# Computing the second row tile's queries, compressed branch and half of its window units beside the last projection chunk

## The chip, the cores and the metric

The kernel runs on one core of a Trainium2 chip. The metric is the device time of one launch in microseconds. Before the change three runs took 1413.13, 1410.7 and 1417.88 us; their median is 1413.13 us. A separate, profiled execution took 1414.72 us.

## What is computed

One transformer block over 1024 positions and 1024 channels, in float32. The normalised input is multiplied with one wide matrix `w_in`; its columns give the parts of two attentions. Attention A has eight heads with dilated windows. Attention B has eight query heads in two groups and three branches per query: a compressed branch (63 pooled keys), a selected branch (the eight best blocks of 64 keys, chosen from the compressed branch's scores) and a local window branch (512 keys back). Cut to what matters here:

```
qa, ka, va, qb, kc, vc, ksl, vsl, kwn, vwn, gl = split_columns(h @ w_in)
p_cmp = masked_softmax(qb @ k_cmp);  o_cmp = p_cmp @ v_cmp
score = overlap(p_cmp) + forced;     idx = top_k(score, 8)
o_sel = softmax over the selected blocks of qb @ ksl, times vsl
o_win = softmax over the last 512 keys of qb @ kwn, times vwn
ob    = gate0 * o_cmp + gate1 * o_sel + gate2 * o_win
h     = x + concat(rms_norm(oa), rms_norm(ob)) @ w_out
out   = rms_norm(h + relu(rms_norm(h) @ w_up)**2 @ w_down)
```

The selected branch needs the compressed branch of the same rows (for the top eight) and the keys and values `ksl`, `vsl`. The window branch needs neither.

## The kernel before

**Stages.** Phase one projects `w_in` in eleven chunks of 256 columns (one has 280) and runs attention A between them. Its order is a list, the string `P1` (line 28): `a0` to `a3` are attention A's head pairs, `kv0`, `qk1`, `v1`, `kw0`, `qb0` and so on are projection chunks, `X` opens attention B's buffers, `kb1` builds the window keys. Near its end stand `Q7` (load and stack the queries of the first row tile), `W7` (its window branch), `C7` (its compressed branch) and, last, `ks0`, the chunk with the selected branch's keys and values. Phase two is the rest of attention B with the output projection, phase three the feed-forward part.

**Order of the work.** The positions are eight row tiles of 128, taken in the order of `ORD` (line 31): tile 5 first, tile 7 second, tile 6 third. The program is written in one order, and a scheduler that runs a model of the engines puts each engine's instructions in an order of its own by priority: a smaller number goes first when it is ready. Chunks are written under `later(LATE)` (line 935), which adds 1000, so what is written after a chunk goes ahead of it where it can, and the chunk's matmuls fill up. Each engine, and the DMA queue of SP with it, then runs its list in order.

**A unit** is one head of one row tile in one branch (`attend`, line 504). It has score matmuls (lines 418, 420), a masked minimum on VectorE (429), an exponential on ScalarE (434), a split into two fp16 halves (448, and 450 on POOL or 452 on VectorE), a DMA that transposes both halves (453) and the matmuls with the values (468 to 470, "PV" below). Up to `DEPB` = 4 units wait for their PV (`retire`, line 485). Row buffers `ns`, halves `hl` and transposed halves `pt` have three slots each; phase two adds a few from the pool `bpp`.

**Around the change.** `q_load` (744) fetches a tile's queries, `q_build` (748) stacks them, `cmp_stages` (755) gives the compressed branch as c1 (matmuls 763 to 766, maximum 775, shift 777, exponential 778), c3 (four transposes, copy 784) and c4 twice (matmuls 795, copy 796, then some thirteen short VectorE steps, 804 to 819). For tile 5 these take slots of `ns` (`big`, line 147). After `ks0`, `wp` and `ht` close, the PSUM pool `ps1` is replaced by `ps3`, `bpp` opens, `build_kb(0)` (949) makes the selected keys, and the loop of line 968 goes over the tiles: first `load_wo` for four rows of `w_out`, then, beside tile n's units, tile n+1's queries and compressed branch at fixed unit counts (`STG`, line 32), then tile n's window and selected branches. Tile 5 has no window branch left there.

**Fillers.** The output projection is cut into pieces. Every unit of attention B adds a rate to a credit (`RATE`, line 39: 0.2 for tile 5, 0.5 for tile 7), and each full credit lets one piece in (`pump`, 876). The credit is set to zero in line 956, just ahead of the loop.

**Large buffers.** The pool `stp` has four slots. At the end of phase one they hold projected columns, afterwards the four pairs of residual rows (`hres`, line 943).

Of the kernel before, what the change touches and what calls it, by code (L numbers as in the profile page):

```python
# [9 lines left out]
F32 = mybir.dt.float32  # L10
# [8 lines left out]
T = 1024  # L19
D = 1024  # L20
NT = 8
# [3 lines left out]
NEG = -1e30  # L25
EPS = 1e-6
PSCALE = 4096.0
P1 = "a0 kv0 qk1 c0 a1 c1 qk2 v1 a2 qk3 kw0 qb0 qb1 a3 X G kb1 Q7 W7 C7 ks0"
CUT = 0
ISS = 0  # L30
ORD = [5, 7, 6, 4, 3, 2, 1, 0]
# [25 lines left out]
def build(tc, A, out):  # L57
# [89 lines left out]
    def big(name="ns", hl=False):  # L147
        if hl:
            return atp[0].tile([128, T], F32, name=name, tag="hl", bufs=3)
        return wk.tile([128, T], F32, name=name, tag="ns", bufs=3)  # L150
# [588 lines left out]
        return bpp.tile(shape, dt, name=name, bufs=bufs)  # L739

    fbn = {}
    Q2 = []

    def q_load(i):
        QR[i] = big("qr0")[:, :512] if i == ORD[0] and "qr" in FB else bpp.tile([128, 512], F32, name="qr", bufs=1)
        sp.dma_start(QR[i], qbd[i])

    def q_build(i):
        q = fb(i, [128, 2, 4, 128], F32R, "qb", 2)
        q2 = Q2[ORD.index(i) % 2]  # L750
        r = QR[i]
        q_stacks(q[:, 0], q[:, 1], q2, [r[:, j * 128:(j + 1) * 128] for j in range(4)])
        QB[i] = (q, q2)

    def cmp_stages(i):
        st = {}

        def c1():
            q, q2 = QB[i]
            ps = bank("S", [128, 512], 3).rearrange("p (h c) -> p h c", c=64)  # L760
            ps = ps.rearrange("p (g j) c -> p j g c", g=2)
            for j in range(4):
                pe.matmul(ps[:, j], identb, cmask[:, i, None, :].to_broadcast([128, 2, 64]), start=True, stop=False)
                for g in range(2):
                    pe.matmul(ps[:, j, g], q2[:, g, j], kcs[:, g], start=False, stop=False)
                    pe.matmul(ps[:, j, g], q[:, g, j], kcs[:, g], start=False, stop=g == 1)
            ps = ps.rearrange("p j g c -> p g j c")
            s = big("cs0")[:, :512].rearrange("p (h c) -> p h c", h=8) if i == ORD[0] and "cs" in FB else bpp.tile([128, 8, 64], F32, name="cs", tag="cs", bufs=1)
            st["s"] = s
            if not CM:  # L770
                dve.tensor_add(s.rearrange("p (g j) c -> p g j c", g=2), ps, cmask[:, i, None, None, :].to_broadcast([128, 2, 4, 64]))
            m = fb(i, [128, 1, 8], F32, "cm", 2)
            st["m"] = m
            x = ps if CM else s.rearrange("p (g j) c -> p g j c", g=2)
            dve.tensor_reduce(m[:, 0].rearrange("p (g j) -> p g j", g=2), x, axis=AX.X, op=OP.max)
            dve.tensor_scalar(m[:, 0], m[:, 0], -1e29, None, op0=OP.max)
            dve.tensor_sub(s.rearrange("p (g j) c -> p g j c", g=2), x, m[:, 0].rearrange("p (g j) -> p g j", g=2)[:, :, :, None].to_broadcast([128, 2, 4, 64]))
            act.activation(s, s, AF.Exp)

        def c3():  # L780
            s = st["s"].rearrange("p h c -> p (h c)")
            ps = transposes([s[:, j * 128:(j + 1) * 128] for j in range(4)])
            pt = big("cpt0")[:, :512].rearrange("p (h c) -> p h c", h=4) if i == ORD[0] and "cs" in FB else bpp.tile([128, 4, 128], F32, name="cpt", bufs=1)
            act.activation(pt, ps, AF.Copy)
            st["pt"] = pt

        def c4(g):
            if g == 0:
                if i == ORD[0] and "cs" in FB:
                    st["e"] = big("ce0")[:, :648].rearrange("p (g a b) -> p g a b", g=2, a=2)  # L790
                else:
                    st["e"] = bpp.tile([128, 2, 2, 162], F32, name="ce", tag="cs", bufs=1)
            ps = bank("O", [128, 512], 1)[:, :324].rearrange("p (a b) -> p a b", a=2)
            for j in range(2):
                pe.matmul(ps[:, j], st["pt"][:, 2 * g + j], vc[:, g], start=True, stop=True)
            act.activation(st["e"][:, g], ps, AF.Copy)
            if g == 0:
                return
            e = st["e"].rearrange("p g a b -> p (g a) b")
            sc = cs2.tile([128, 2, 2, 16], F32, name="csc", bufs=2)  # L800
            mx = cs2.tile([128, 8], F32, name="cmx", bufs=2)
            im = cs2.tile([128, 8, 16], F32, name="cim", bufs=1)
            rd = cs2.tile([128, 2, 4, 2], F32, name="crd", bufs=2)
            dve.tensor_scalar(rd[:, 0], e[:, :, 128:130], 1e-30, None, op0=OP.max)
            dve.reciprocal(rd[:, 0], rd[:, 0])
            dve.tensor_mul(im.rearrange("p (a b) s -> p a b s", a=4),
                           e[:, :, 130:162].rearrange("p a (b s) -> p a b s", b=2),
                           rd[:, 0, :, :, None].to_broadcast([128, 4, 2, 16]))
            dve.tensor_reduce(sc[:, 0], im.rearrange("p (g h) s -> p g s h", g=2), axis=AX.X, op=OP.add)
            OC[i] = fb(i, [128, 8, 64], F32, "oc", 3)  # L810
            dve.tensor_mul(rd[:, 1], rd[:, 0], gate[:, i, 0:24:3].rearrange("p (a b) -> p a b", a=4))
            pool.tensor_mul(OC[i].rearrange("p (a b) d -> p a b d", a=4),
                            e[:, :, 0:128].rearrange("p a (b d) -> p a b d", b=2),
                            rd[:, 1, :, :, None].to_broadcast([128, 4, 2, 64]))
            dve.tensor_add(sc[:, 0], sc[:, 0], addt[:, i, None, :].to_broadcast([128, 2, 16]))
            for g in range(2):
                dve.max(mx, sc[:, 0, g])
                dve.match_replace(sc[:, 1, g], mx, sc[:, 0, g], NEG)
            dve.tensor_scalar(sc[:, 1], sc[:, 1], -1.0, NEG, op0=OP.mult, op1=OP.add)
            for g in range(2):  # L820
                SB[i, g] = sc[:, 1, g]

        return c1, c3, lambda: c4(0), lambda: c4(1)

    def b_attend(i, br):
        n0 = max(0, i - 4)
        if br == 0:
            OB[i] = wop.tile([128, 8, 64], F32, name="ob", bufs=3)

        def f(br, h):  # L830
            g, j = divmod(h, 4)
            q, q2 = QB[i]
            if h == 0:
                OT[i, br] = fb(i, [128, 8, 65], F32, "ot", 2)
            k = kb[br][:, g].rearrange("p a b -> p (a b)")
            a, n = (0, i + 1) if br == 0 else (n0, i + 1 - n0)
            u = dict(i=i, h=h, q=q[:, g, j], q2=q2[:, g, j], k=k[:, a * 128:], n=n,
                     v=lambda t: V["kw" if br else "ks"][:, a + t, g], ev=OT[i, br][:, h - 1:h + 1], e=h % 2)
            if br:
                u["tab"] = wint[:, (5 - n) * 128:]  # L840
            else:
                u["sc"] = SB[i, g]
            return u

        for h in range(8):
            u = f(br, h)
            if h == 7:
                u["done"] = lambda: b_done(i, br)
            attend(u)
# [40 lines left out]
    for step in P0:  # L890
        if step == "X":
# [13 lines left out]
            ctmp = big()  # L905
            addt = bqp.tile([128, NT, 16], F32, name="addt")
            Q2.append(q2_tile(bqp, "qb20"))
            sp.dma_start(ctmp[:, :512], A["cmask"].rearrange("p a b -> p (a b)"))
            dve.tensor_copy(cmask.rearrange("p a b -> p (a b)"), ctmp[:, :512])
            sp.dma_start(addt, A["addt"])  # L910
# [12 lines left out]
        if step == "C7":  # L923
            for f in cmp_stages(ORD[0]):
                f()
            continue
        k, j = step[:-1], int(step[-1])
        if k == "a":
            a_pair(j)
# [10 lines left out]
    ps1_close()  # L940
    pst["pool"], ps3_close = mkpool("ps3", space=PSUM)
    pst["second"] = 1
    hres += [stp.tile([128, 2, T], F32, name="st") for j in range(4)]
    bpp, bpp_close = mkpool("bpp", side="right")
    Q2.append(q2_tile(bpp, "qb21"))
    for tag in ("ns", "hl", "pt"):
        xtra[tag] = (bpp, 0)
    kb[0] = bpp.tile([128, 2, NT, 128], F32R, name="kb0")
    build_kb(0)
    if "Q7" not in P0:  # L950
        q_load(ORD[0])
        q_build(ORD[0])
    if "C7" not in P0:
        for f in cmp_stages(ORD[0]):
            f()
    credit[0] = 0.0

    eng = dict(P=mybir.EngineType.PE, A=mybir.EngineType.Activation, D=mybir.EngineType.DVE, G=mybir.EngineType.Pool, S=mybir.EngineType.SP)
# [9 lines left out]
    for n, i in enumerate(ORD):  # L968
        if n == 0:
            load_wo(range(4))  # L970
        if n + 1 < NT:
            q_load(ORD[n + 1])
            jobs = (lambda i=ORD[n + 1]: q_build(i),) + cmp_stages(ORD[n + 1])
            for k, f in zip(STG, jobs):
                waiting.append([k, f])
        if n or "W7" not in P0:
            b_attend(i, 1)
        b_attend(i, 0)
    retire(0)
# [339 lines left out]
```

## Time and profile before

| | |
|---|---|
| median of three runs | 1413.13 us |
| the profiled execution's own time | 1414.72 us |
| its span, first to last instruction | 1412.9 us |
| matmuls on TensorE (PE) | busy 1313.4 us, 93% |
| weight loads on TensorE (PEld) | busy 1110.6 us, 79% |
| VectorE (DVE) | busy 970.4 us, 69% |
| ScalarE (ACT) | busy 650.3 us, 46% |
| GpSimd (POOL) | busy 512.0 us, 36% |

Busy shares are means over stages with different limits, and a matmul's record covers its whole way through the array, so that records of successive matmuls overlap. What a stage allows is read from the stretch itself: the idle time of each engine there, the granted clock of TensorE (1.00 is 2.4 GHz, and a mean below it means that part of the stretch ran at 1.2 GHz), and the chain of waits.

### The profile page before, as it was taken

To read this page: it belongs to the slowest core of one execution; us is meant where nothing else is said; L and a number is where in the kernel's file an instruction comes from. 1 tells how busy PE (TensorE), PEld (TensorE's weight loads), DVE (VectorE), ACT (ScalarE), POOL (GpSimd) and SP (SyncE) were. 2 spreads that over 40 slices of the span, in tenths; PEclk is the share of its full clock that TensorE was granted. 3 is DMA by queue.
4 is the path that set the end of the run, shared out by engine and by line. 5 is a ranking of instruction groups with operands and counts; after the bars stand their busy time and mean duration, and the time that the engine had idled before them with its cause. 6 is when DMAs were issued, how large, how long until landed. Compare 5 with 4: busy or idle time off the path is not lost.

```text
span 1412.9 us, 23742 instructions
## 1 busy us (share of the span) xinstructions
PE 1313.4 (93%) x8891; PEld 1110.6 (79%) x8891; DVE 970.4 (69%) x1953; ACT 650.3 (46%) x1212; POOL 512.0 (36%) x724
## 2 busy tenths in 40 slices
PE   7999999998987999899778999999999999999996
PEld 6788989888976777677656888888888888788885
DVE  6664565773458876878587667677767667776767
ACT  7462755872557866898553222222222212222216
POOL 3445473664445665577542110011111001111115
PEclk9999999999898999999999999999999999999998
DMA  6265382985538986686311121112111111111113
GB/s 189 68 113 120 87 185 51 206 184 145 93 107 180 172 152 129 143 157 96 82 30 34 56 59 46 45 46 60 45 60 46 59 41 50 55 50 61 45 46 134
DMA packets 265747, 131.68 MB, mean 93 GB/s; under 512 B 220064, under 2 KB 240544, under 8 KB 265632
## 3 DMA queue, kind: packets, MB, share of 16 engines
q1 hardware_dynamic: 265488, 129.90, 40.0%
q8 instruction: 70, 1.15, 0.3%
q14 instruction: 45, 0.37, 0.1%
q10 hardware_dynamic: 144, 0.26, 0.0%
HBM read 68.26 MB, written 8.39 MB: 54 GB/s over the span
## 4 chain that ended last, share of the span: by engine, by line
PE 57%; DVE 16%; DMA 8%; issue 7%; POOL 6%; ACT 5%; SPq 1%; DVEq 0%; POOLq 0%; ACTq 0%
PE S L1124 8%; PE S L1125 7%; PE S L1126 7%; PE F L335 3%; PE F L336 3%; PE F L337 3%; DMA u<-in_w_down_dram 3%; PE O L1064 2%; PE O L1063 2%; PE T L1065 2%; PE T L1063 2%; PE T L1064 2%; PE O L1065 2%; PE S L418 2%; DVE c L1071 1%
## 5 line engine op out<-in xcount | busy, mean ns | idle before, releaser
L1073 POOL TENSOR_TENSOR ul<-c,uh 128x512 fp32r<-128x512 f32 x64 | 92.5, 1454 | 557.8 <-ACT uh L1072 555.9
L1127 DVE SCALAR_TENSOR_TENSOR st<-S,r,st 128x512 f32<-128x512 f32 (+1 forms) x257 | 185.8, 742 | 70.3 <-PE S L1126 69.7
L1124 PE MATMUL S<-dn,uh 128*128 128x512 f32 (+1 forms) x514 | 203.2, 396 | 9.6 <-DVE c L1110 5.9
L1126 PE MATMUL S<-dn,ul 128*128 128x512 f32 (+1 forms) x514 | 200.6, 391 | 0.8 <-POOL ul L1073 0.8
L1125 PE MATMUL S<-dn,uh 128*128 128x512 f32 (+1 forms) x514 | 200.8, 391 | 0.0
L335 PE MATMUL F<-wh,hh 128*128 128x256 f32 (+1 forms) x576 | 167.2, 292 | 6.1 <-DVE st L214 3.2
L336 PE MATMUL F<-wl,hh 128*128 128x256 f32 (+1 forms) x576 | 166.5, 289 | 2.3 <-DVE wl L95 2.3
L337 PE MATMUL F<-wh,hl 128*128 128x256 f32 (+1 forms) x576 | 165.4, 288 | 0.0
L1124 PEld LDWEIGHTS S<-dn,uh 128*128 128x128 f32 x514 | 97.2, 189 | 37.8 <-DVE c L1110 12.2
L434 ACT ACTIVATE ns<-ns,mn 128x640 f32<-128x640 f32 (+7 forms) x152 | 110.7, 747 | 35.1 <-POOL mn L433 21.7
L335 PEld LDWEIGHTS F<-wh,hh 128*128 128x128 f32 x576 | 110.7, 193 | 8.2 <-DVE st L214 3.6
L450 POOL TENSOR_TENSOR hl<-ns,hl 128x640 f16<-128x640 f32 (+5 forms) x67 | 105.5, 1575 | 30.9 <-ACT hl L448 24.9
L1126 PEld LDWEIGHTS S<-dn,ul 128*128 128x128 f32 x514 | 97.0, 189 | 22.0 <-POOL ul L1073 1.5
L336 PEld LDWEIGHTS F<-wl,hh 128*128 128x128 f32 x576 | 111.3, 193 | 3.7 <-DVE wl L95 3.1
L1125 PEld LDWEIGHTS S<-dn,uh 128*128 128x128 f32 x514 | 97.4, 190 | 19.2
L337 PEld LDWEIGHTS F<-wh,hl 128*128 128x128 f32 x576 | 111.0, 193 | 0.5
L448 ACT ACTIVATE hl<-ns 128x640 f16<-128x640 f32 (+5 forms) x115 | 91.2, 802 | 5.8 <-DMA pt<-hl 5.0
L468 PE MATMUL O<-v,pt 128*128 128x65 f16 x694 | 77.3, 195 | 15.9 <-DMA pt<-hl 13.4
L1081 ACT ACTIVATE c<-T 128x512 f32<-128x512 f32 x15 | 9.0, 599 | 172.2 <-PE S L1125 172.2
L468 PEld LDWEIGHTS <-pt 128*128 128x128 f16 x694 | 63.9, 99 | 27.6 <-DMA pt<-hl 17.4
L418 PE MATMUL S<-kb,qb 128*128 128x384 f32 (+3 forms) x192 | 72.9, 385 | 12.6 <-DVE mn L429 8.9
L433 POOL TENSOR_SCALAR mn<-mn 128x1 f32<-128x1 f32 x130 | 43.7, 336 | 96.4 <-DVE mn L429 81.2
(372 smaller groups left out, 3625.1 us busy)
## 6 DMA issues: line engine op xcount, KB each, us to landing
u<-in_w_down_dram SPq DMA_DIRECT2D x64, 256.0 KB, 2.8
wr<-in_w_in_dram SPq DMA_DIRECT2D x44, 256.0 KB, 2.9
r<-in_w_up_dram SPq DMA_DIRECT2D x32, 256.0 KB, 2.7
st<-in_x_dram SPq DMA_DIRECT2D x8, 512.0 KB, 5.9
wor<-in_w_out_dram SPq DMA_DIRECT2D x16, 256.0 KB, 3.5
cA<-in_w_up_dram SPq DMA_DIRECT2D x16, 256.0 KB, 2.8
cB<-in_w_up_dram SPq DMA_DIRECT2D x16, 256.0 KB, 2.6
ns<-in_xT_dram SPq DMA_DIRECT2D x7, 512.0 KB, 5.1
```

The costliest lines, as they stand in the source:

```text
L335: pe.matmul(ps, hh[:, k, ts], hi, start=k == 0, stop=False)
L336: pe.matmul(ps, hh[:, k, ts], lo, start=False, stop=False)
L337: pe.matmul(ps, hl[:, k, ts], hi, start=False, stop=k == KD - 1)
L418: pe.matmul(ps[:, :w], u["q"], u["k"][:, cs], start=True, stop=False)
L434: u["exp"] = act.activation(ns[:, :n * 128], ns[:, :n * 128], AF.Exp, scale=-1.0, bias=mn[:, j:j + 1])
L450: pool.tensor_sub(lo, p, hi)
L468: pe.matmul(ps, ph, v[:, 64:129], start=t == 0, stop=False)
L1073: pool.tensor_sub(lo, a, f32(hi))
L1124: pe.matmul(ps, uh[:, ts], wd[:, 0, cs], start=j == 0, stop=False)
L1125: pe.matmul(ps, uh[:, ts], wd[:, 1, cs], start=False, stop=False)
L1126: pe.matmul(ps, ul[:, ts], wd[:, 0, cs], start=False, stop=j == 1)
L1127: dve.scalar_tensor_tensor(o[:, cs], ps, r2[:, t:t + 1], o[:, cs], op0=OP.mult, op1=OP.add)
```

## The change

`P1` gets three steps ahead of `ks0`. `QN` loads and stacks the queries of tile 7, `CN` computes its compressed branch, `WN` its window branch for heads 0 to 3. Heads 4 to 7 are written after `build_kb(0)` and before the credit is set to zero. The loop then prepares tile n+1 only from n = 1 on and leaves out tile 7's window branch. For this, tile 7's stacked queries and its outputs (`EX`) lie in two slots of `stp`; the residual rows are allotted in the order 2, 3, 1, 0; the second `q2` tile moves from `bpp` to `bqp`, a pool of phase one; the compressed branch of both tiles takes `ns` slots; `cm` moves to `cs2`, and `crd` has one buffer instead of two. Cut to its core:

```diff
-P1 = "a0 kv0 qk1 c0 a1 c1 qk2 v1 a2 qk3 kw0 qb0 qb1 a3 X G kb1 Q7 W7 C7 ks0"
+P1 = "a0 kv0 qk1 c0 a1 c1 qk2 v1 a2 qk3 kw0 qb0 qb1 a3 X G kb1 Q7 W7 C7 QN CN WN ks0"
...
     def q_load(i):
-        QR[i] = big("qr0")[:, :512] if i == ORD[0] and "qr" in FB else bpp.tile([128, 512], F32, name="qr", bufs=1)
+        QR[i] = big("qr0")[:, :512] if i in ORD[:2] else bpp.tile([128, 512], F32, name="qr", bufs=1)
...
     def q_build(i):
-        q = fb(i, [128, 2, 4, 128], F32R, "qb", 2)
+        if i == ORD[1]:
+            q = stp.tile([128, 2, 4, 128], F32R, name="st")
+        else:
+            q = fb(i, [128, 2, 4, 128], F32R, "qb", 2)
...
-            rd = cs2.tile([128, 2, 4, 2], F32, name="crd", bufs=2)
+            rd = cs2.tile([128, 2, 4, 2], F32, name="crd", bufs=1)
...
-    def b_attend(i, br):
+    def b_attend(i, br, heads=range(8)):
...
             Q2.append(q2_tile(bqp, "qb20"))
+            Q2.append(q2_tile(bqp, "qb21"))
...
+        if step == "QN":
+            q_load(ORD[1])
+            ex = stp.tile([128, 1032], F32, name="st")
+            EX.append(ex[:, 0:520].rearrange("p (h d) -> p h d", d=65))
+            EX.append(ex[:, 520:1032].rearrange("p (h d) -> p h d", d=64))
+            q_build(ORD[1])
+            continue
+        if step == "CN":
+            for f in cmp_stages(ORD[1]):
+                f()
+            continue
+        if step == "WN":
+            b_attend(ORD[1], 1, range(4))
+            continue
...
-    hres += [stp.tile([128, 2, T], F32, name="st") for j in range(4)]
+    rows = {j: stp.tile([128, 2, T], F32, name="st") for j in (2, 3, 1, 0)}
+    hres += [rows[j] for j in range(4)]
     bpp, bpp_close = mkpool("bpp", side="right")
-    Q2.append(q2_tile(bpp, "qb21"))
...
     build_kb(0)
...
+    b_attend(ORD[1], 1, range(4, 8))
     credit[0] = 0.0
...
-        if n + 1 < NT:
+        if 0 < n < NT - 1:
             q_load(ORD[n + 1])
...
-        if n or "W7" not in P0:
+        if n > 1:
             b_attend(i, 1)
         b_attend(i, 0)
```

## Rows read from the trace of the kernel before

**Rows 1.** The page: busy time of each engine over the span.

```profile
PE 1313.4 (93%) x8891; PEld 1110.6 (79%) x8891; DVE 970.4 (69%) x1953; ACT 650.3 (46%) x1212; POOL 512.0 (36%) x724
```

**Rows 2.** By stretch: length, busy PE, PEld, DVE, ACT, POOL (instructions), PE clock, DMA.

```profile
...
366.00:382.00 16.00, 13.80 (x127) 13.14 (x127) 8.83 (x30) 11.62 (x28) 9.24 (x17) 0.76 0.70 129
382.00:405.50 23.50, 23.50 (x195) 23.49 (x193) 6.67 (x24) 8.06 (x21) 10.19 (x33) 0.94 0.22 29
405.50:420.50 15.00, 9.31 (x99) 6.55 (x97) 12.27 (x33) 10.78 (x21) 6.17 (x13) 1.00 0.80 251
420.50:440.50 20.00, 16.34 (x135) 13.92 (x135) 14.79 (x31) 15.11 (x23) 8.04 (x8) 0.74 0.75 141
440.50:460.00 19.50, 15.47 (x187) 13.14 (x188) 18.48 (x56) 15.78 (x29) 12.54 (x15) 1.00 0.86 181
540.00:600.00 60.00, 50.72 (x497) 39.60 (x495) 45.47 (x123) 43.85 (x77) 31.47 (x38) 1.00 0.69 135
...
```

**Rows 3.** Chain that ended last, 405 to 427 us: start, duration, what.

```profile
...
409.65 5.20 DMA qr<-qbd
...
```

**Rows 4.** The same chain, 440 to 460 us: first and last of 63 pieces.

```profile
...
440.31 0.92 ACT ns L434
...
458.57 0.39 PE S L418
...
```

**Rows 5.** PE, timeline: start, duration, what; counts are each instruction's.

```profile
...
353.96 0.60 PE L360 MATMUL T<-c_ident,qr 128*128 128x128 f32 x4
354.32 0.36 PE L336 MATMUL F<-wl,hh 128*128 128x256 f32 x1
...
374.33 0.34 PE L337 MATMUL F<-wh,hl 128*128 128x256 f32 x1
...
376.62 0.33 PE L763 MATMUL S<-cmask,identb 128*128 128x128 bf16 x1
...
380.15 0.26 PE L468 MATMUL O<-v,pt 128*128 128x65 f16 x1
...
382.05 0.56 PE L335 MATMUL F<-wh,hh 128*128 128x256 f32 x1
...
391.98 0.71 PE L795 MATMUL O<-vc,cpt 128*128 128x162 f32 x4
392.42 0.39 PE L337 MATMUL F<-wh,hl 128*128 128x256 f32 x1
...
456.75 0.20 PE L468 MATMUL O<-v,pt 128*128 128x65 f16 x1 [1.05 <-DMA pt<-hl]
...
457.21 0.42 PE L418 MATMUL S<-kb,qb 128*128 128x384 f32 x1
...
457.88 0.34 PE L418 MATMUL S<-kb,qb 128*128 128x384 f32 x1
...
```

**Rows 6.** VectorE, timeline: one window unit, and ends of c4's steps for tile 5.

```profile
...
396.57 0.17 DVE L804 TENSOR_SCALAR crd<-ce 128x8 f32<-128x8 f32 x1 [2.76 <-ACT ce L796]
...
399.84 0.18 DVE L819 TENSOR_SCALAR csc<-csc 128x32 f32<-128x32 f32 x1
...
438.06 0.55 DVE L429 CUSTOM_DVE_ANT_0 nsx<-S,wint 128x384 f32<-128x384 f32 x1
...
438.77 0.48 DVE L429 CUSTOM_DVE_ANT_0 nsx<-S,wint,mn 128x256 f32<-128x256 f32 x1 [0.15 <-PE O L795]
...
451.77 0.81 DVE L452 SCALAR_TENSOR_TENSOR hl<-ns,hl 128x640 f16<-128x640 f32 x1
...
```

**Rows 7.** The tile qb: the second query split on VectorE (min/median/max ns).

```profile
...
L383 DVE SCALAR_TENSOR_TENSOR qb<-T,qb x8: 694/695/695, 357.8 to 648.3; 64x512 fp32r<-64x512 f32 x8
...
```

**Rows 8.** SP's queue, waits 366 to 410 us: total, times, longest.

```profile
...
SPq L453 <- PE O L470: 24.3, 2, 21.6
...
```

**Rows 9.** SP's queue, timeline of the same stretch.

```profile
...
407.49 1.17 SPq L681 DMA_DIRECT2D oat<-oad  x2
...
```

**Rows 10.** Line 709 of the output projection: durations ns min/median/max, first and last start.

```profile
...
L709 PE MATMUL F<-woh,mh x128: 387/395/796, 420.5 to 707.5; 128*128 128x512 f32 x128
...
```

More of the change, by code (lines that the diff above doesn't have):

```diff
@@ L741, in build @@
     fbn = {}
-    Q2 = []
+    Q2, EX = [], []
     def q_load(i):
-        QR[i] = big("qr0")[:, :512] if i == ORD[0] and "qr" in FB else bpp.tile([128, 512], F32, name="qr", bufs=1)
+        QR[i] = big("qr0")[:, :512] if i in ORD[:2] else bpp.tile([128, 512], F32, name="qr", bufs=1)
         sp.dma_start(QR[i], qbd[i])
     def q_build(i):
-        q = fb(i, [128, 2, 4, 128], F32R, "qb", 2)
+        if i == ORD[1]:
+            q = stp.tile([128, 2, 4, 128], F32R, name="st")
+        else:
+            q = fb(i, [128, 2, 4, 128], F32R, "qb", 2)
         q2 = Q2[ORD.index(i) % 2]
@@ L767, in c1 @@
             ps = ps.rearrange("p j g c -> p g j c")
-            s = big("cs0")[:, :512].rearrange("p (h c) -> p h c", h=8) if i == ORD[0] and "cs" in FB else bpp.tile([128, 8, 64], F32, name="cs", tag="cs", bufs=1)
+            s = big("cs0")[:, :512].rearrange("p (h c) -> p h c", h=8) if i in ORD[:2] else bpp.tile([128, 8, 64], F32, name="cs", tag="cs", bufs=1)
             st["s"] = s
@@ L771, in c1 @@
                 dve.tensor_add(s.rearrange("p (g j) c -> p g j c", g=2), ps, cmask[:, i, None, None, :].to_broadcast([128, 2, 4, 64]))
-            m = fb(i, [128, 1, 8], F32, "cm", 2)
+            m = cs2.tile([128, 1, 8], F32, name="cm", bufs=2)
             st["m"] = m
@@ L782, in c3 @@
             ps = transposes([s[:, j * 128:(j + 1) * 128] for j in range(4)])
-            pt = big("cpt0")[:, :512].rearrange("p (h c) -> p h c", h=4) if i == ORD[0] and "cs" in FB else bpp.tile([128, 4, 128], F32, name="cpt", bufs=1)
+            pt = big("cpt0")[:, :512].rearrange("p (h c) -> p h c", h=4) if i in ORD[:2] else bpp.tile([128, 4, 128], F32, name="cpt", bufs=1)
             act.activation(pt, ps, AF.Copy)
@@ L788, in c4 @@
             if g == 0:
-                if i == ORD[0] and "cs" in FB:
+                if i in ORD[:2]:
                     st["e"] = big("ce0")[:, :648].rearrange("p (g a b) -> p g a b", g=2, a=2)
@@ L809, in c4 @@
             dve.tensor_reduce(sc[:, 0], im.rearrange("p (g h) s -> p g s h", g=2), axis=AX.X, op=OP.add)
-            OC[i] = fb(i, [128, 8, 64], F32, "oc", 3)
+            OC[i] = EX[1] if i == ORD[1] else fb(i, [128, 8, 64], F32, "oc", 3)
             dve.tensor_mul(rd[:, 1], rd[:, 0], gate[:, i, 0:24:3].rearrange("p (a b) -> p a b", a=4))
@@ L823, in cmp_stages @@
         return c1, c3, lambda: c4(0), lambda: c4(1)
-    def b_attend(i, br):
+    def b_attend(i, br, heads=range(8)):
         n0 = max(0, i - 4)
-        if br == 0:
+        if br == 0 and 0 in heads:
             OB[i] = wop.tile([128, 8, 64], F32, name="ob", bufs=3)
@@ L833, in f @@
             if h == 0:
-                OT[i, br] = fb(i, [128, 8, 65], F32, "ot", 2)
+                OT[i, br] = EX[0] if (i, br) == (ORD[1], 1) else fb(i, [128, 8, 65], F32, "ot", 2)
             k = kb[br][:, g].rearrange("p a b -> p (a b)")
@@ L843, in f @@
             return u
-        for h in range(8):
+        for h in heads:
             u = f(br, h)
@@ L949, in build @@
     build_kb(0)
[L950 to L955, printed above, removed]
+    b_attend(ORD[1], 1, range(4, 8))
     credit[0] = 0.0
```

## The prediction

> **What bounds the kernel now.** First the page: PE is busy for 93% of the span [rows 1], so over the whole kernel there is little idle time to win, and the change adds and removes no matmul of weight. The question is therefore not how much work moves but how well the two stretches on either side of the chunk's end are filled. So the second view is the busy time by stretch [rows 2]. Between 366 and 382 us tile 5's window units and its compressed branch run beside the start of the last chunk; PE is busy 13.80 of 16.00 us at a mean clock of 0.76. From 382 to 405.5 us the chunk runs alone: PE 23.50 of 23.50, while VectorE is busy 6.67 us and ScalarE 8.06. Then phase two starts badly: PE 9.31 of 15.00 us, then 16.34 of 20.00 at clock 0.74, then 15.47 of 19.50, and in this last stretch VectorE is busy 18.48 of 19.50. The reader is to see that one side has PE full and VectorE empty, and the other the reverse.
>
> The third view is the chain that ended last. Right after the chunk it goes through tile 7's query load, 5.20 us [rows 3], which is just what the change takes away from there. From 440.31 to 458.57 us it runs on ScalarE and VectorE alone [rows 4], so that work taken from these two should shorten that stretch directly.
>
> **The change, term by term.**
>
> *Work that moves, on PE.* I use start-to-start times at full clock, since the records overlap [rows 5]. Four query transposes: 354.32 - 353.96 = 0.36 us, and as much for c3. c1 has 20 matmuls; in tile 5 nineteen of them took 380.15 - 376.62 = 3.53 us in the slow part of that stretch, which at full clock I estimate at half, so 1.9 for all. c4: 392.42 - 391.98 = 0.44, twice, 0.9. Scores of one unit: 457.88 - 457.21 = 0.67, four units 2.7. PV of one unit: 457.21 - 456.75 = 0.46; four, 1.8. These four are tile 5's last PVs, which now are written before the chunk because four more units follow them, while tile 7's first four take their place behind it. Sum 8.0 us.
>
> *On VectorE.* Query splits 0.7 us each, two: 1.4 [rows 7]. c1: a reduction and a shift over as many columns, taken as equal to a split, and a small step, 1.5. c4: 13 steps from 396.57 to 400.02, 3.4 with the gaps [rows 6]. A unit's minima: 0.55 + 0.48 and two read-outs of 0.08, 1.2; four units 4.8. One or two of four units split their halves on VectorE, 0.81 each [rows 6], 1.2. Sum 12.3 us. ScalarE's part I take as of the same size: an exponential of about 0.9 us [rows 4] and a copy of like width per unit, beside the four query copies and those of c1 to c4.
>
> *(a) Taken from 405.5 to 460 us.* Low bound 0: other waits could fill the place. High bound: VectorE's 12.3 us over its share of that time, (12.27 + 14.79 + 18.48) / 54.5 = 0.84, is 14.6. PE's own 8.0 lies between. I take 12, near VectorE's sum, because the chain at the end of that stretch is VectorE and ScalarE work [rows 4], and the query DMA stands on the chain too [rows 3]. **-12.**
>
> *(b) Added to 366 to 405.5 us.* VectorE's 12.3 us and ScalarE's share lie in their idle time there (39.5 - 15.5 us on VectorE [rows 2]), so they cost nothing while PE is the cover. PE's 8.0 us has no cover from 382 on. Before that there is some: PE is idle for 2.2 us, and a mean clock of 0.76 over 16 us gives away 3.8, in all 6.0. From 374.33 to 382.05 no matmul of the chunk started [rows 5]. Bounds: 2.0 if all of that is recovered, 8.0 if none is, and 8.0 + 7.7 = 15.7 if a second such hole appears for tile 7. I take half recovered, between the even cases: **+5.0.** The Trainium skill, page Perfetto Trace Analysis, section Identifying the Most-Contended Engine, says that matmul occupancy is a poor measure of headroom and that weight-load occupancy is to be used. The trace gives 23.49 of 23.50 us for weight loads in that stretch, so by that rule nothing is recovered, (b) would be +8.0, and the time 1407.6. I stay with half, since the lost 6.0 us lie before 382.
>
> *(c) Tile 7's other four window units.* They stay behind the chunk but need nothing from it, so they can run while the selected keys are built. PE is idle 5.7 us from 405.5 to 420.5 [rows 2]. Bounds 0 and -5.7; their scores alone are 2.7 us: **-2.5.**
>
> *(d) Fillers.* Eight units of tile 7 no longer add credit after the reset: 8 x 0.5 = 4 pieces come later. A half-row piece has 12 matmuls of at most 0.395 us [rows 10], so under 4.8 us, and of four pieces three are such. By the rates and blocks of the code they catch up in tile 4, where PE is idle 9.3 of 60 us [rows 2]; that idle time covers them, and if it is gone they cost up to 14 us. I take **+1**, since more than half of the idle time there would have to be unusable before they cost much.
>
> *(e) Queues and buffers.* The query load of tile 7 is one DMA more before the chunk and one fewer after it. SP's queue is already blocked there: a transpose waits 21.6 us for a PV that stands behind the chunk [rows 8], and the loads of phase two start only when it has gone, at 407.49 [rows 9]. The change moves that block from tile 5's last unit to tile 7's fourth; behind it wait the same loads, so 0, between -1 and +3. Residual rows 0 to 3 must now wait for tile 7's buffers; by the credits their first load comes a unit before or after these are free, 0 to +2, taken as 0. The zeroing of the second `q2` moves out of the start of phase two, at most -0.9 us of VectorE, taken with (a). One `crd` buffer: its next writer is a tile later, 0.
>
> Sum: -12 + 5.0 - 2.5 + 1 = -8.5 us. Against the profiled execution, 1414.72 us (its span of 1412.9 and 1.8 around it), that is 1406.2. This execution stands 1.6 us above the median of the runs, so against 1413.13 I forecast **1404.6 us**. About 0.5% (7 us) is what a measurement of this kernel can tell from no change.
>
> **Rivals.**
>
> *The chunk takes it back.* PE was full there, all 8.0 us and part of a second hole are paid, and (a) gives only PE's 8.0. Without the hole 1413.13 - 8.0 + 8.0 - 2.5 + 1 = 1411.6, with half of it 1415.5; say **1412**. For it: PE and weight loads at 23.5 of 23.5. Against: the clock of 0.76 just before. It is also what comes out if the scheduler puts `CN` and `WN` behind the chunk after all, so that nothing runs beside it.
>
> *Slower: two serial chains through three row slots.* Tile 5's compressed branch took from its first matmul at 376.62 [rows 5] to 400.0 us [rows 6], its steps lying between chunk matmuls. Tile 7's takes its query load and three further tiles from the same three `ns` slots as the window units. If it can only follow, it ends near 376.6 + 2 x 23.4 = 423 us, and units and the chunk's evacuations on the same in-order engines wait with it. The start of phase two then slips by 18 us, less 12 and plus 1: +7, **1420**. It decides once the chunk ends more than 14 us later than 405.5. Against it: VectorE and ScalarE are two thirds idle there.
>
> *Larger gain.* The first 35 us of phase two lose their gap and with it the slow clock that follows it: 0.26 x 20 = 5.2 us more [rows 2], (c) reaches -5.7, and (b) is 2.0. Then 1413.13 - 12 - 5.2 - 5.7 + 2.0 + 1 = **1393**. The Trainium skill, page TensorE: Matmul & The Clock Gate, Part 1 (The HAM clock gate), says that idle time lowers the clock to 1.2 GHz; the trace agrees in order, with the gap at 405.5 and the mean of 0.74 behind it.
>
> **How the numbers follow.** Forecast case 0.52 (its own range 1399 to 1410), the chunk takes it back 0.2, slower 0.14, larger gain 0.14. The range over all, 1391 to 1418, takes in the larger gain with (a) near its high bound, and leaves out the slower case past its middle and the tail of the larger gain, about a tenth on each side. Faster by over 0.5% (below 1406.1): 0.4 of the forecast case's 0.52, and 0.14, gives 0.54. Slower by over 0.5%: 0.14 and a rest of the second case, 0.15. Within: 0.31.
>
> **What would show it.** (a) The stretch from the chunk's end to the end of tile 5's selected units is shorter and no query load stands on its chain. (b) The last projection matmul starts between 408 and 414 us instead of 405.3, with compressed matmuls of two tiles before it. (c) Window scores of tile 7 lie between the chunk's end and the first selected score. (d) PE is busier between tile 6 and tile 4's end. The forecast is wrong if the chunk ends after 420, if the gap at its end is as long as before, or if later stretches give back more than 4 us.

## The result and the profile after

The changed kernel is **slower by 1.2%**: 1435.18 us against 1415.46 us (medians of four runs each), a ratio of 1.0116 with a 95% interval from 1.0085 to 1.0147. Later runs gave 1.0119 (1.0082 to 1.0155). The prediction, 1404.6 us with a range of 1391 to 1418, was wrong in direction and range.

The profiled execution took 1436.04 us with a span of 1434.3. The page's line of busy times, with the same 8891 matmuls as [rows 1]:

```profile
...
PE 1331.3 (93%) x8891; PEld 1126.5 (79%) x8891; DVE 974.1 (68%) x1953; ACT 650.4 (45%) x1212; POOL 508.8 (35%) x724
...
```

PE's share is unchanged; its busy time grew by 18 us with no new work, which goes with a lower clock: 0.963 over the span and not 0.980. The same stretches as [rows 2] (columns as there):

```profile
...
366.00:382.00 16.00, 13.33 (x117) 12.63 (x116) 9.35 (x32) 12.54 (x29) 9.44 (x18) 0.84 0.70 137
382.00:405.50 23.50, 23.50 (x198) 23.50 (x196) 7.80 (x26) 10.18 (x25) 9.49 (x31) 0.89 0.27 40
405.50:420.50 15.00, 12.49 (x135) 10.60 (x133) 10.79 (x29) 10.78 (x23) 5.13 (x12) 1.00 0.55 161
420.50:440.50 20.00, 15.78 (x100) 11.85 (x101) 16.93 (x49) 14.65 (x24) 11.20 (x13) 0.66 1.04 239
440.50:460.00 19.50, 15.55 (x176) 11.76 (x177) 12.07 (x32) 12.26 (x19) 12.08 (x12) 0.91 0.89 176
540.00:600.00 60.00, 55.55 (x580) 47.00 (x579) 43.98 (x124) 45.80 (x77) 33.05 (x40) 0.94 0.79 143
...
```

The gap behind the chunk did fill: 12.49 us of PE in 15.00, where [rows 2] have 9.31. VectorE did get freer from 440.5 to 460: 12.07 us against 18.48. But PE did not gain by it: 100 matmuls in the 20 us from 420.5, where there were 135, at a clock of 0.66, and 176 against 187 in the next stretch. So the load that left the vector engines behind 440.5 us did not turn into progress of PE.

Less work went ahead of the chunk's end than the change intends. Of tile 7, four query transposes, the 20 matmuls of c1 and 5 score matmuls start there. Its compressed branch is done at 423.3 us, and tile 5's last window outputs are copied at 417.91 and 422.46, where before it was at 406.52 and 410.18. VectorE's busy time from 366 to 405.5 us is 17.15 us and was 15.50. Start, duration and what, in the changed kernel:

```profile
...
398.78 0.60 PE L360 MATMUL T<-c_ident,qr 128*128 128x128 f32 x4
...
417.91 0.27 ACT L475 ACTIVATE ot<-O 128x130 f32<-128x130 f32 x1
...
421.99 1.34 DVE L822 TENSOR_SCALAR csc<-csc 128x32 f32<-128x32 f32 x1
...
422.46 0.28 ACT L475 ACTIVATE ot<-O 128x130 f32<-128x130 f32 x1
...
```

Idle time of PE behind the chunk is what output-projection pieces fill. Busy PE by stretch for line 711 alone, a third of their matmuls; first the kernel before, then the changed one:

```profile
...
420.00:460.00 40.00, 3.99 (x8) 1.94 (x8) 0.87 0.79 159
460.00:500.00 40.00, 9.13 (x23) 4.33 (x24) 1.00 0.95 178
500.00:540.00 40.00, 6.77 (x17) 3.19 (x17) 1.00 0.80 143
540.00:580.00 40.00, 7.39 (x18) 3.42 (x18) 1.00 0.70 137
580.00:620.00 40.00, 5.51 (x14) 2.63 (x14) 1.00 0.78 151
...
```

```profile
...
420.00:460.00 40.00, 3.62 (x8) 1.80 (x8) 0.79 0.96 209
460.00:500.00 40.00, 3.24 (x8) 1.52 (x8) 0.83 0.88 164
500.00:540.00 40.00, 7.32 (x18) 3.87 (x19) 0.96 0.89 173
540.00:580.00 40.00, 10.18 (x26) 4.70 (x25) 1.00 0.83 139
580.00:620.00 40.00, 2.10 (x6) 1.14 (x6) 0.79 0.70 146
...
```

Read the counts: from 420 to 460 us there are 8 in both, so the slow stretch at 420.5 us is not theirs (a second profile of the changed kernel has a clock of 0.83 there, and 118 matmuls). From 460 to 500 us there are 8 of these matmuls and not 23: this is the hole that the pieces leave. They come back between 540 and 580, and then, from 580 to 620, there are 6 instead of 14, at a clock of 0.79. The code gives a reason for this second hole, a dependency: the load of the second half of `w_out` is itself an entry in the list of pieces, behind all of the first half. In the timeline its last weight is split at 612.1 us, and at 592.1 before.

Two other things stand out. The chain that ended last now crosses tile 7's selected units on two transposes (start, duration, what):

```profile
...
490.74 0.95 ACT hl L448
...
491.77 8.02 DMA pt<-hlx
...
500.90 5.73 DMA ptx<-hl
...
```

SP's timeline shows what was issued just ahead of the first one:

```profile
...
489.57 0.57 SPq L681 DMA_DIRECT2D oat<-oad  x1
490.19 0.42 SPq L746 DMA_DIRECT2D qr<-qbd  x1
490.66 0.90 SPq L682 DMA_DIRECT2D st<-in_x_dram  x2
491.77 5.23 SPq L453 DMA_TRANSPOSE pt<-hlx  x1
...
```

Two residual-row loads of 512 KB are under way when the transpose starts. Before, six of the eight row loads started from 270.1 to 285.2 us and two at 410; now four start at 418 to 421, two at 490.7 and two from 514. The last four come once two of the row slots, which tile 7's queries and output buffers hold, are free (PE last reads these queries at 485.9 us); why the first four come so late was not followed up. The long transpose is one event: in the second profile none between 405 and 530 us took more than 6.6 us to land, and before none more than 5.4.

And the MLP, which no line of the diff touches, has a wait of PE that the kernel before does not have:

```profile
...
PE O L1076 <- ACT wb L94: 5.6, 7, 1.0
...
```

Three marks split the executions: the end of the last projection matmul, the first matmul of the MLP's up projection, and the end. Before: 405.5 us, then 303.8, then 703.6. After: 409.6, then 315.2, then 709.5. So of the 21.4 us between the two spans 4.1 lie ahead of the chunk's end, 11.4 in attention and output projection, and 5.9 in the MLP.

### The profile page after: what moved, and what is told of

It reads as the page before. It is cut to its first block, busy times and chain, and to the rows that moved or that the text cites. A ratio compares the mean times of both kernels' runs of the same rounds, so it can differ in the third digit from the quotient of the medians.

```text
span 1434.3 us, 23754 instructions
## 1 busy us (share of the span) xinstructions
PE 1331.3 (93%) x8891; PEld 1126.5 (79%) x8891; DVE 974.1 (68%) x1953; ACT 650.4 (45%) x1212; POOL 508.8 (35%) x724
## 4 chain that ended last, share of the span: by engine, by line
PE 56%; DVE 13%; DMA 11%; ACT 7%; issue 6%; POOL 5%; SPq 1%; POOLq 0%; DVEq 0%; ACTq 0%
PE S L1137 7%; PE S L1138 7%; PE S L1139 7%; PE F L335 3%; PE F L336 3%; PE F L337 3%; DMA u<-in_w_down_dram 3%; DMA pt<-hl 2%; DVE c L1084 2%; PE T L1076 2%; PE T L1077 2%; PE T L1078 2%; PE O L1076 2%; PE S L418 2%; PE O L1077 2%
## 5 line engine op out<-in xcount | busy, mean ns | idle before, releaser
L1086 POOL TENSOR_TENSOR ul<-c,uh 128x512 fp32r<-128x512 f32 x64 | 89.8, 1412 | 565.9 <-ACT uh L1085 491.5
L1140 DVE SCALAR_TENSOR_TENSOR st<-S,r,st 128x512 f32<-128x512 f32 (+1 forms) x257 | 189.4, 745 | 111.8 <-PE S L1139 111.3
L450 POOL TENSOR_TENSOR hl<-ns,hl 128x640 f16<-128x640 f32 (+5 forms) x68 | 109.9, 1617 | 42.0 <-ACT hl L448 35.7
L468 PE MATMUL O<-v,pt 128*128 128x65 f16 x699 | 81.5, 199 | 28.2 <-DMA pt<-hl 15.5
L470 PE MATMUL O<-v,pt 128*128 128x65 f16 x699 | 80.7, 199 | 0.0
L469 PE MATMUL O<-v,pt 128*128 128x64 f16 x699 | 80.6, 198 | 0.0
```

The source lines that it names most:

```text
L450: pool.tensor_sub(lo, p, hi)
L468: pe.matmul(ps, ph, v[:, 64:129], start=t == 0, stop=False)
L1086: pool.tensor_sub(lo, a, f32(hi))
L1140: dve.scalar_tensor_tensor(o[:, cs], ps, r2[:, t:t + 1], o[:, cs], op0=OP.mult, op1=OP.add)
```

## The experiments

Four theories. **A**: tile 7's chain does not fit beside the chunk, and its window units then stand in the way of tile 5's selected units. **B**: late row loads crowd the transposes. **C**: the credits of tile 7's eight window units are lost, so pieces come late and PE idles. **D**: the static order that the scheduler wrote is a bad one by chance. "Behind the chunk" below is the time from the last projection matmul to the first up matmul in a run's profile (before 303.8, after 315.2).

### Credits back in the changed kernel, and out of the kernel before

```
-RATE = [0.2, 0.5, 0.6, 1.0, 0.3, 0.5, 0.1, 0.6]
+RATE = [0.2, 1.0, 0.6, 1.0, 0.3, 0.5, 0.1, 0.6]   (changed kernel)
+RATE = [0.2, 0.25, 0.6, 1.0, 0.3, 0.5, 0.1, 0.6]  (kernel before)
```

> The changed kernel with one number altered: the credit rate of tile 7 is 1.0 in place of 0.5, so that its eight selected units alone add the 8 credits that its sixteen units added before. Theory A: within 4 us of the changed kernel, some 20 us above before. Theory B: the same, within 4 us of the changed kernel. Theory C: 8 to 15 us faster than the changed kernel, that is 5 to 12 us above before.

> The kernel before with one number altered: the credit rate of tile 7 is 0.25 in place of 0.5, so that its sixteen units add 4 credits fewer, as many as the change takes away. Theory A and theory B: within 3 us of before. Theory C: 8 to 12 us slower than before. The prediction's term for it was 1 us, with a bound of 14.

Measured: the changed kernel with its credits back is at **0.9969** (0.9954 to 0.9985), some 21 us below itself and faster than before. The kernel before with the same four credits missing is at **1.0006** (0.9991 to 1.0022). The first exceeds what C foresaw, the second contradicts it. The first kernel's pieces (line 711 again) are back in their places:

```profile
...
460.00:500.00 40.00, 7.91 (x20) 3.76 (x20) 1.00 1.00 196
500.00:540.00 40.00, 7.91 (x20) 3.77 (x20) 1.00 0.87 166
540.00:580.00 40.00, 7.45 (x19) 3.57 (x19) 1.00 0.83 148
580.00:620.00 40.00, 6.31 (x15) 2.98 (x15) 0.96 0.86 151
...
```

Behind the chunk it takes 294.3 us. Tile 5's window units still end at 431.2 us, as in the changed kernel (416.0 before), so theory A's late chain is there in full and yet costs nothing: A falls.

### Only queries and compressed branch moved

```
-P1 = "... Q7 W7 C7 QN CN WN ks0"
+P1 = "... Q7 W7 C7 QN CN ks0"
```

The four later units go back behind tile 5's selected units too.

> The changed kernel without the four early window units: tile 7's queries and compressed branch stay beside the last chunk, all its eight window units go back behind tile 5's selected units and add credit again. The two row slots stay taken, so the row loads come late as in the changed kernel. Theory A (serial chain, and the window units ahead of tile 5's selected units in the start of phase two): tile 5's selected units end about where they did before (416 us and not 431), and the time is within 5 us of before, or below it. Theory B: as slow as the changed kernel but for 4 us. Theory C: between them, 8 to 12 us faster than the changed kernel, since the credits are back.

Measured 1.0019 (0.9997 to 1.0040). (The 416 and 431 us of the expectation are the ends of tile 5's window units, not of its selected ones.) A's milestone was missed: they ended at 429.0 us. The run gives the credits back as well. Its time lies where A allowed it and some 14 us below the changed kernel, past the 8 to 12 of C.

### How much credit, and when

```
RATE[1], changed kernel:  0.5 -> 0.75,  0.5 -> 1.25;   RATE[2]: 0.6 -> 0.85
RATE[1], kernel before:   0.5 -> 0.75
```

> The changed kernel with tile 7's credit rate halfway between its 0.5 and the 1.0 that brought the time back: 0.75, so that its eight selected units add 6 credits where the changed kernel adds 4 and the kernel before added 8. Theory C (the missing pieces leave PE idle behind the chunk, and its clock falls): halfway, 5 to 13 us above before, as one piece is some 5 us of PE. Theory D (the order that the scheduler happened to write for the changed kernel is a bad one, and any other order frees it): within 4 us of the kernel with 1.0, that is at or below before. Theory A: as the changed kernel, 15 to 20 us above before.

> The changed kernel with tile 7's credit rate at 1.25, 10 credits where before had 8. Theory C (PE has idle time there that takes a piece for nothing until it is full): at the level of the rate 1.0, within 3 us. Theory D (chance of the order): anything between that and the changed kernel. The kernel before with 4 credits more was 0.5% slower, so this may be too, by up to 7 us.

> The changed kernel with the lost 4 credits given back a tile later: tile 6's rate is 0.85 in place of 0.6 over its sixteen units, tile 7's stays at 0.5. If the pieces are needed beside tile 7's selected units: tile 7's selected units still end near 514 us, and the time is no more than 8 us below the changed kernel. If it only matters that they are done before the second half of the output projection can begin: at the level of before, within 4 us.

> The kernel before with tile 7's credit rate at 0.75 in place of 0.5, so that its sixteen units add 12 credits, 4 more than before. It asks whether the 0.3% by which the changed kernel with its credits restored beat the kernel before belongs to the moved work or to pieces that simply come earlier. If it is the moved work: within 3 us of before. If it is the earlier pieces: 4 to 6 us faster than before.

Measured, in the changed kernel: 4 credits 1.0119, 6 credits **1.0073** (1.0049 to 1.0097), 8 credits 0.9969, 10 credits **0.9968** (0.9949 to 0.9987). Four credits given back a tile later: **1.0060** (1.0036 to 1.0085), half of the loss. The 6 credits lie halfway, as C foresaw and D did not. Of the later credits it isn't settled whether the place counts: tile 7's selected units ended at 503.1 us and not near 514, the milestone that was set for it. The kernel before with four credits more is *slower*, 1.0050 (1.0025 to 1.0075): the 0.3% that the restored kernels win is not simply that pieces come earlier.

### Row loads

First attempt: dummy tiles in two row slots of the kernel before, and the rows allotted in the changed order.

```
+HOLD.append(stp.tile([128, 1032], F32, name="st"))   (twice, behind C7)
+rows = {j: stp.tile([128, 2, T], F32, name="st") for j in (2, 3, 1, 0)}
```

> The kernel before, with only the residual-row loads changed: two dummy tiles hold two of the row slots until tile 7's selected units are written, and the rows are allotted in the changed kernel's order, so that six of the eight half-megabyte row loads move from phase one into the crowded stretch behind the chunk. All arithmetic of the outputs is that of before. Theory A (tile 7's chain does not fit beside the chunk, and its window units then stand ahead of tile 5's selected units): within 3 us of before, since nothing of that order is changed. Theory B (the row loads now run among the transposes of tiles 5 and 7 and delay them): 8 to 15 us slower than before. Theory C (eight units of tile 7 no longer add credit, so output-projection pieces come later and PE has too little beside the attention): within 3 us of before.

Measured 0.9987 (0.9973 to 1.0001), but it tells nothing of B: the dummies were written and read at once, and the loads ran from 268.8 to 284.5 and at 405 us as before. The second attempt ties the dummies to tile 4's query load; its companion takes the loads out of the changed kernel.

```
+if i == ORD[3]:
+    for x in HOLD:
+        pool.tensor_add(x[:, 1:2], x[:, 0:1], r[:, 0:1])

-sp.dma_start(hr(i), A["x"][i * 128:(i + 1) * 128, :])
+pool.memset(hr(i), 0.0)
```

> The first attempt at theory B again, since there the dummy tiles were let go at once and the row loads stayed where they were. Here a GpSimd step that needs tile 4's query load reads and writes both dummies, so they hold their two slots up to about 490 us, as tile 7's queries do in the changed kernel, and six of the eight row loads move behind the chunk. Theory B: 6 to 15 us slower than before. Theories A, C and D: within 4 us of before.

> The changed kernel without the eight residual-row loads: GpSimd fills the row tiles with zeros instead, so the residual input is left out of the output. Theory B (the loads crowd the transposes behind the chunk): at least 8 us faster than the changed kernel. Theory C: within 4 us of the changed kernel, since the credits are still missing. Theory D: the order differs, so anything between before and the changed kernel.

Measured: held slots in the kernel before **1.0026** (1.0006 to 1.0045), with loads at 411 to 413 and 444.6 to 446.4 us; no loads in the changed kernel 1.0076 (1.0053 to 1.0100), some 6 us below it. So B alone falls short: 4 us where it foresaw 6 to 15, and 6 where it foresaw 8 or more. The 4 us are less than an order alone moves (below), and the intervals of the 6 overlap. Nor is the first run a full copy: its slots came free by 444.6 us, where tile 7's queries and outputs hold theirs to about 490 and 514 us.

### Dummy matmuls in the places of the lost pieces

```
+if u["i"] == ORD[1] and "sc" in u and u["h"] % 2:
+    with later(100):
+        pinned(u, lambda: dummy(u))      (12 matmuls of 512 columns, nobody reads them)
```

> The changed kernel with 12 dummy matmuls of 512 columns (a piece's worth of PE work, written to an output-projection bank that nobody reads) behind every second selected unit of tile 7: four in all, in the places of the four pieces whose credit was lost. The real pieces stay as late as in the changed kernel. Theory C1 (without the pieces PE idles, its clock falls, and the slow clock holds up the attention itself): the clock loss between the chunk's end and 515 us falls from 17 to 6 us or less, tile 7's selected units end at some 506 us and not 514, and the time is 4 to 10 us below the changed kernel, since the pieces are still late. Theory C2 (the clock is only a sign; the loss is the late pieces' own 19 us of PE work): no faster than the changed kernel, or up to 5 us slower.

> The changed kernel unaltered, for more executions of it beside these three, since its first four lay between 1425 and 1438 us. Every theory: 10 to 21 us above before.

The dummy kernel came to 1.0088 (1.0057 to 1.0118), the changed kernel beside it to 1.0119 (1.0082 to 1.0155): 4 us apart, and the intervals overlap, so C1 is not decided by the time. The clock is higher, as C1 said. From 409 to 520 us (length, busy PE, PEld, DVE, ACT, POOL, clock, DMA), the changed kernel's first profile, its second, and the dummy's:

```profile
...
409.00:520.00 111.00, 91.13 (x883) 72.67 (x883) 76.86 (x210) 75.51 (x122) 58.55 (x65) 0.85 0.90 185
...
```

```profile
...
409.00:520.00 111.00, 89.96 (x954) 71.75 (x953) 79.60 (x224) 81.58 (x135) 57.87 (x69) 0.94 0.96 198
...
```

```profile
...
409.00:520.00 111.00, 97.24 (x1025) 78.64 (x1024) 82.37 (x226) 80.99 (x130) 62.28 (x67) 0.97 0.95 199
...
```

The first two are the same program: 883 matmuls at a mean clock of 0.85, or 954 at 0.94. The second profile ended at 1427.1 us, 7.2 earlier. So a lower clock goes with part of the first profile's excess, and it differs from one execution to the next; what remains in the second, 14.2 us over before, is in both. Nor does the clock decide C1: reckoned from the chunk's end (404.6 us with the dummies, 409.6 without) the mean over 110 us is 0.84, 0.94 and 0.97, and tile 7's selected units end 104.3, 97.7 and 97.8 us behind it. The dummies bring them no sooner than the second profile of the unaltered kernel has them.

### Both losses together in the kernel before, and orders

Neither missing credits (1.0006) nor late rows (1.0026) cost the kernel before more than 0.3%. Together:

```
held slots as above, and
-RATE = [0.2, 0.5, ...]     or, in the other run, in pump:
+RATE = [0.2, 0.25, ...]    +if u["i"] != ORD[1] or "sc" in u:   (no credit from window units)
```

> The kernel before with two losses together: the row slots held to about 490 us as in the run that was 0.26% slower, and tile 7's rate at 0.25, which alone was 0.06% slower. If the two only add: 1 to 8 us above before. If late row loads and missing pieces work on one another (theory B times C): 10 to 20 us above before, as the changed kernel.

> The kernel before with the credits lost in the place where the changed kernel loses them: tile 7's eight window units add none, its eight selected units 0.5 each, so that no piece comes due between tile 5's and tile 7's selected units. If the place of the loss is what costs: 8 to 18 us above before. If the loss is cheap as long as the window units themselves are there to fill PE: within 4 us of before, as with the rate of 0.25.

> The pair again in the kernel before, with the credits lost where the changed kernel loses them (no credit from tile 7's window units: 1.0005 alone) and the row slots held (1.0026 alone). If missing pieces and late row loads work on one another: 9 to 21 us above before, as in the first pair. If the first pair was chance of the order: 0 to 9 us above before.

Measured: held slots with a rate of 0.25 **1.0131** (1.0098 to 1.0164). No credit from the window units alone 1.0005 (0.9984 to 1.0026); with held slots **1.0070** (1.0055 to 1.0085). The sums of the single losses would be 1.0032 and 1.0031. The same stretch for the kernel before, for no credit from window units, and for the two pairs:

```profile
...
409.00:520.00 111.00, 96.31 (x969) 78.22 (x970) 91.50 (x238) 86.83 (x141) 61.69 (x67) 0.95 0.86 176
...
```

```profile
...
409.00:520.00 111.00, 96.73 (x969) 79.81 (x970) 91.12 (x239) 85.53 (x136) 63.14 (x67) 0.92 0.88 170
...
```

```profile
...
409.00:520.00 111.00, 88.00 (x858) 71.62 (x859) 81.63 (x212) 75.62 (x123) 56.36 (x64) 0.87 0.84 180
...
```

```profile
...
409.00:520.00 111.00, 89.68 (x866) 74.16 (x865) 81.03 (x215) 76.73 (x126) 58.24 (x65) 0.85 0.83 176
...
```

The pairs show the mark of the changed kernel's first profile (883 at 0.85): 858 and 866 matmuls, at a clock of 0.87 and 0.85, where before and the run without credit from window units have 969 and the rate of 0.25 alone has 982 at 0.92. Held slots alone lie between, with 914 at 0.89. And the second half of `w_out`: its last split comes 206.8 and 199.2 us behind the chunk's end in the pairs, 202.5 and 195.2 in the changed kernel's two profiles, but 186.6 before, and 177.5 to 188.7 in the kernels with either loss alone.

How much of this is chance of the order, two runs tried by an edit that takes nothing away, in both kernels, and a third with the credits back:

```
-STG = (1, 5, 7, 8, 9)
+STG = (2, 6, 8, 9, 10)
```

> The changed kernel with the five steps of every next tile's queries and compressed branch due one unit later (2, 6, 8, 9, 10 in place of 1, 5, 7, 8, 9). It takes no credit and no load away, but another order comes out. Theory C: 10 to 20 us above before, as the changed kernel. Theory D (a bad order by chance): anything from before up, most likely 0 to 8 us above before.

> The same edit in the kernel before, to show how far an order alone moves the time. Theory C: within 5 us of before. Theory D: the spread of orders is of the size of the loss itself, so 5 to 15 us away from before in either direction, more likely slower, as the kernel before had been tuned.

> The changed kernel with both edits: tile 7's rate at 1.0 and the five steps of the next tiles due one unit later. If restored credits are what counts: below the changed kernel with the later steps alone (1.0063), between 0.995 and 1.002 of before. If the 1.0 kernel was merely a lucky order: no better than 1.0063.

Measured: changed kernel 1.0063 (1.0040 to 1.0086), kernel before 1.0051 (1.0029 to 1.0072), changed kernel with credits back 1.0043 (1.0029 to 1.0057). An order alone is worth 7 to 8 us either way. For the changed kernel, 8.9 us above before, C had foreseen 10 to 20 and D most likely 0 to 8. And with later steps in both kernels the change itself costs nothing that can be told, 1.0063 against 1.0051: the 1.2% belong to one order. In this order the credits bring 0.2% only, between the two outcomes that were set. Nor does the changed kernel with later steps show the mark of the weights, which come 186.6 us behind its chunk.

| | rows early | rows late |
|---|---|---|
| full credit | before 1; later steps 1.0051 | held 1.0026; changed, credits back 0.9969 and 0.9968, with later steps 1.0043; queries and branch only 1.0019 |
| four credits missing | 1.0006; 1.0005 | changed 1.0119, with later steps 1.0063; pairs 1.0131, 1.0070 |

(The run without row loads, 1.0076, stands in no cell: its GpSimd fills still wait for the slots.) The four kernels with both losses average 1.0096, all others in the table lie within about 0.5% of before. So both losses together stand above either alone in all four kernels, which supports an interaction. It isn't shown apart from the order, which moves a kernel by 0.5%, and by which the same credits were worth 1.5% or 0.2%; theory D has a part in the loss that no run here separates.

## Why the prediction was wrong

**(d) Fillers: the step that failed.** The prediction said of the idle time in tile 4 that it "covers them, and if it is gone they cost up to 14 us. I take **+1**". The credits back took the kernel from 1.0119 to 0.9969, 21 us, which is well beyond what an order alone moved; in the order with later steps they brought 3 us. Two things were not in the sum. First, the step looked only at where the pieces would be caught up, and not at the stretch that they leave: there PE had too little in their place, 883 or 954 matmuls against 969, and in the first profile its clock fell to 0.85 (0.94 in the second, 0.95 before). Second, the catching up did happen, as forecast (26 of line 711's matmuls from 540 to 580 us, before 18), but the load of the second weights waits behind the last caught-up piece, and came 20 us later (12.7 in the second profile), so the next pieces were late as well.

**(e) Row loads, "0 to +2, taken as 0".** They cost 1.0026 in the kernel before, about 4 us, within what an order alone moves. Credits missing alone cost 1 us there, just what (d) said, and only with late rows did they become dear. So as far as the pairs show, what was wrong is that the two were priced apart. Why late rows make missing pieces dear was not settled, and how much of it is the order stays open. That PE waits more often for a transpose behind the row loads, and has no piece at hand for it, was only argued; the chain at 490 us shows such a wait in the changed kernel's first profile.

**(b) +5.0 ahead of the chunk's end: the number came out, by luck.** The chunk ended at 409.6 us, 4.1 later, inside 408 to 414. But half of 8.0 us was not recovered. Of what was to move, the query transposes, c1 and 5 of the 16 score matmuls of the four early units ran there, at the prediction's own prices some 3.1 us; c3, c4, the other scores and tile 5's last PVs ran behind the chunk. The hole in the chunk's matmuls ahead of 382 us, 7.7 us long before, is again 7.5 us long (from 375.9). Nor is 4.1 a figure to 1 us: in the nine profiles without early steps the chunk ended between 397.7 and 408.2 us, in the ten with all of them between 404.6 and 413.4. The rule set beside it, of the Trainium skill, Perfetto Trace Analysis, Identifying the Most-Contended Engine, would have made it +8.0; since most of that work ran elsewhere, 4.1 decides neither for nor against it.

**(a) and (c), together -14.5: right in sign at best.** With the credits back the time behind the chunk fell from 303.8 to 294.3 and, at 10 credits, 295.7 us, so -8 to -9.5; but with later steps it was 304.8, +1.0. Taken to the first up matmul, where the spread of the chunk's end drops out, these three stand at 704.1, 703.1 and 713.4 us, before at 709.3. Of (a), less than half of the relief came: from 405.5 to 460 us VectorE is busy 39.8 us in the changed kernel and was 45.5, 5.7 less where 12.3 were priced. PE's gain did not follow by itself. (c) was seen: PE 12.49 us against 9.31 in the gap. The MLP, 5.9 us longer, had no term at all; that later stretches give back more than 4 us was one of the prediction's signs of being wrong.

**The rivals.** "The chunk takes it back" gave 1412, also for the case that the steps fall behind the chunk; most of them did, yet the loss came from elsewhere. "Two serial chains" gave 1420 and came nearest, for another reason. Its place was right, and so was its time: tile 7's compressed branch was done at 423.3 us, where it said 423. VectorE's timeline shows tile 7's compressed maximum and its first window minimum around the chunk's end:

```profile
...
407.51 0.69 DVE L778 TENSOR_REDUCE cm<-S 128x8 f32<-128x512 f32 x1 [4.15 <-PE S L769]
...
410.65 0.56 DVE L429 CUSTOM_DVE_ANT_0 ns<-S,wint 128x384 f32<-128x384 f32 x1 [0.44 <-PE T L360]
...
```

So the window units, but for some scores, ran behind the chunk and not beside it. Its price was wrong: the chunk slipped by 4.1 us and not by over 14, and the kernel with credits back has the same chain and is fast. "Larger gain" named the clock behind the gap; the gap was filled, and the clock fell all the same, to 0.66 from 420.5. The rule that the prediction set beside it, from the Trainium skill, TensorE: Matmul & The Clock Gate, Part 1 (The HAM clock gate), is that idle time lowers the clock to 1.2 GHz. The traces do not speak against it: from 409 to 520 us the mean clock is 0.97 with dummy matmuls in the lost pieces' places, and 0.85 or 0.94 without. But the two profiles of one program, 0.85 and 0.94, lie further apart than 0.94 and 0.97.

## What to carry to other kernels

When work is moved out of a stretch, list what it paced there: here every attention unit also bought filler work for PE, and moving the unit silently removed the filler, with a weight load queued behind it. Then look in the trace whether the work did move: most of it had not. Price two side effects that meet in one stretch together, and change the pacing along with the move (here one number, 0.5 to 1.0, turned 1.2% slower into 0.3% faster, though in another order it brought 0.2%). Before a single measurement is explained by its mechanism, shift something neutral in the same kernel: if that alone moves the time by 0.5%, smaller differences can't be put down to the mechanism, and a larger one is to be tried in a second order too.

## What was not expected

**The MLP's order changes with edits 200 us ahead of it.** In the changed kernel ScalarE's split of `wb` stands behind that of `wa` in every second block; before, it stood ahead. PE then waits 5.0 to 6.8 us in all for `wb`, in six to eight waits, in 11 of the 20 profiles, and 2.3 us or less in the others. With it the MLP takes 704.1 to 710.0 us, without it 701.2 to 705.7; so 5 to 6 us of the changed kernel's loss lie there, and that much of it is chance of the written order. It isn't the whole: no credit from the window units alone has the same wait and costs nothing that can be told.

**The clock differs between executions of the same instructions.** Before and with a rate of 0.25 the kernels have the same order on PE up to well behind the chunk, yet the chunk ended at 405.5 us in one profile and at 397.7 in the other; the mean clock from 366 to 382 us was 0.76 in the first and 1.00 in the second.
